# Writing the split parts of 41 weight units to DRAM in the first block and reading them back in the other three

## The chip, the core and the metric

The kernel runs on one core of one Trainium2 chip. The metric is the device time of one execution in microseconds; the time before is 2770.3 us, the median of three runs (2768.29 to 2771.04).

## What is computed

One layer of a streaming encoder on 2048 frames of width 1024, all in float32. One combined projection of the input `h` feeds two branches, which are gated, merged and projected again:

```python
(q_a, k_a, v_a, z_a, beta_a, dec_a, q_b, k_b, v_b, z_b, gate_a, gate_b) = split(h @ w_in)
o_a = gated_deltanet(q_a, k_a, v_a, beta_a, dec_a, conv_w, a_log, dt_bias)   # conv, chunked triangular solve
y_a = rms_norm(o_a) * silu(z_a)
y_b = sliding_window_sink_attention(q_b, k_b, v_b, sinks) * silu(z_b)
mixed = sigmoid(gate_a) * (y_a @ w_proj_a) + sigmoid(gate_b) * (y_b @ w_proj_b)
out = layer_norm(ALPHA * h + mixed @ w_out)
```

The triangular solve of the DeltaNet branch needs, for each pair of heads, the inverse of small lower triangular matrices; the kernel makes it on GpSimd.

## The kernel before

**Tiling.** The 2048 frames are worked in four blocks of 512 columns, one after the other. Each block needs all weights once. A weight unit is 128x1024 float32 (512 KB; the first three of a block, "tm", are a little smaller), and a block uses 93 units in a fixed order, `wlist`: three "tm" units, 38 units of the DeltaNet branch and of the first attention group (convolutions of k, q and v, the z gates, k of the attention), which makes 41, then 12 units of attention, 32 of gates and branch projections and eight of the output projection. The order repeats in every block, and so do loads and splits.

**Split.** A float32 product is made of three fast ones. A unit `wr` is split into a high part `wh` (ScalarE, line 248) and a low part `wl` = `wr` - `wh` (line 142: on VectorE, or on GpSimd for the units in `on_pool`, which all come after the first 41). TensorE then takes `wh` with both parts of the input and `wl` with the high part, 24 matmuls of 512 columns a unit (line 275, 16 with `wh` first, then eight with `wl`).

**Buffers and order.** The pool `wp` has two buffers each for the tags `wr`, `wh` and `wl`. When unit i is taken (`get_w`), the load of unit i+2 is issued on SyncE's queue (SP, line 236), and the split of unit i+1 is begun: ScalarE at once, VectorE three ticks later, a tick being six matmuls. In the first block the k, q and v units also use `wr` itself for the meta tokens (line 281), and their next load is issued in the middle of the unit. All DMAs go through SP's one queue, which issues in program order and stops at a wait.

**What runs beside it.** Two generators are advanced at fixed rates between groups of six matmuls: `chain` (the DeltaNet recurrence, `stage_c`, then attention) and `side` (its preparation, `stage_b0` to `stage_b2`). So the order on every engine is fixed when the program is built. For each of four groups g of two heads, `stage_b1` makes `LT` on VectorE (lines 756 to 763); `inverse` writes pieces of it to DRAM (line 777), reads them back in another layout (781), runs 31 steps of two instructions on GpSimd (789, 791), writes the result to DRAM (797) and reads it back as `XT` (802). `stage_c` starts with a transpose of `XT` on VectorE (854) and matmuls that read it (867, 877). Convolutions are three VectorE instructions (668) with a Tanh on ScalarE (671) and a product (673) behind them. `norm` of the block before (1257, 1259, 1261, 1263) still runs at the start of a block.

Of the kernel before, what the change touches and what calls it, by code (L numbers as in the profile page):

```python
# [11 lines left out]
F32 = mybir.dt.float32  # L12
F32R = mybir.dt.float32r
# [23 lines left out]
CONV = (2, 1, 1)  # L37
DMA = (1, 3, 4, 1, 2, 4)
COLS = 2

GS = (26, 9)
NG = 6
# [4 lines left out]
def weight_order(nblk):  # L47

    fm = lambda *us: [("fm", u) for u in us]
    conv = lambda g: [base + 2 * g + i for base in (U_KA, U_QA, U_VA) for i in range(2)]  # L50
    z = lambda g: [U_ZA + 2 * g, U_ZA + 2 * g + 1]
    swa = lambda kv: [base + 2 * kv + i for base in (U_QB, U_ZB) for i in range(2)]
    r, pool = [], set()
    for b in range(nblk):
        r += [("tm", i) for i in range(3)] + fm(*conv(0), U_KB, U_KB + 1)
        for g in range(4):
            r += fm(*(conv(g + 1) if g < 3 else swa(0)), *z(g))
        n = len(r)
        for kv in range(1, KV):
            r += fm(*swa(kv))  # L60
        for v in range(NG):
            r += fm(U_GA + v, U_GB + v, U_PA + v)
        pool.update(range(n, len(r)))
        r += fm(*(U_PB + v for v in range(NG)))
        for v in range(NG, 8):
            r += fm(U_GA + v, U_GB + v, U_PA + v, U_PB + v)
        r += [("wo", i) for i in range(8)]
    return r, pool
# [3 lines left out]
def hybrid_kernel(  # L72
# [26 lines left out]
    V, A, G, T, SY = nc.vector, nc.scalar, nc.gpsimd, nc.tensor, nc.sync  # L99
    seq = xtok.shape[0]  # L100
    nblk = seq // TB

    cp = ctx.enter_context(tc.tile_pool(name="cp", bufs=1))
    wp = ctx.enter_context(tc.tile_pool(name="wp", bufs=2))
# [6 lines left out]
    dp = ctx.enter_context(tc.tile_pool(name="dp", bufs=1, space=bass.MemoryType.DRAM))  # L111
# [4 lines left out]
    def nm(s):  # L116
        cnt[0] += 1
        return f"{s}_{cnt[0]}"

    def g4(shape, dt=F32):  # L120
        return gp.tile(shape, dt, tag="g", name=nm("g"))
# [17 lines left out]
    f = lambda ap: ap.bitcast(F32)  # L139
    def split_lo(out_, src, hi, pool=False):  # L140
        eng = G if pool else V
        eng.tensor_tensor(out=out_, in0=src, in1=f(hi), op=ALU.subtract)  # L142
# [22 lines left out]


    wlist, on_pool = weight_order(nblk)
    raws, parts = {}, {}
    state = {"dma": 0, "split": 0, "use": 0, "more": 0}

    def w_src(key):
        if key[0] == "tm":
            n = 2 if key[1] == 2 else 3
            return wtm[:, 3 * key[1]:3 * key[1] + n, :], [P, n, 272]
        if key[0] == "wo":
            return wo[key[1] // 4, :, 2 * (key[1] % 4):2 * (key[1] % 4) + 2, :], [P, 2, 512]
        return wfm[key[1]], [P, NK, P]
# [5 lines left out]
    def bg(gen, after=0):  # L183

        if after:
            clock["n"] += 1
            heapq.heappush(waiting, (clock["now"] + after, clock["n"], gen))
            return
        try:
            r = next(gen)  # L190
        except StopIteration:
            return
        if callable(r):
            def poll(r=r):
                while not r():
                    yield 3
                bg(gen)
            bg(poll())
            return
        bg(gen, r)  # L200
# [30 lines left out]
    def next_dma():  # L231
        i = state["dma"]
        if i < len(wlist) and i < state["use"] + state["more"] + 2:
            src, shape = w_src(wlist[i])
            raw = wp.tile(shape, F32, tag="wr", name=nm("wr"))
            SY.dma_start(out=raw, in_=src)
            raws[i] = (raw, shape)
            state["dma"] += 1

    def next_split():  # L240
        i = state["split"]
        if i >= len(wlist) or i >= state["use"] + state["more"] + 1:
            return
        state["split"] += 1
        raw, shape = raws.pop(i)
        keep = i >= len(wlist) - 4
        hi = g4(shape, F32R) if keep else wp.tile(shape, F32R, tag="wh", name=nm("wh"))
        A.activation(hi, raw, AF.Copy)  # L248
        lo = g4(shape, F32R) if keep else wp.tile(shape, F32R, tag="wl", name=nm("wl"))
        parts[i] = (hi, lo, raw)  # L250
        if i in on_pool:
            split_lo(lo, raw, hi, True)
            return
        if i:
            yield LO
        split_lo(lo, raw, hi)

    def get_w(key, keep=False):
        i = state["use"]
        assert wlist[i] == key, (wlist[i], key)  # L260
        state["use"] += 1
        if not keep:
            next_dma()
        bg(next_split())
        hi, lo, raw = parts.pop(i)
        return (hi, lo, raw) if keep else (hi, lo)

    def proj(u, rh, rl, done, meta=None):

        wh, wl, raw = get_w(("fm", u), True) if meta is not None else (*get_w(("fm", u)), None)  # L270
        ps = bank(pa)
        n = 0
        for w_, rs in ((wh, (rh, rl)), (wl, (rh,))):
            for k, r_ in ((k, r_) for k in range(NK) for r_ in rs):
                T.matmul(ps, w_[:, k, :], r_(k), start=(n == 0), stop=(n == 3 * NK - 1))  # L275
                n += 1
                if meta is not None and n == 12:
                    pm = bank(pa)
                    for k_ in range(NK):
                        a = 32 * (k_ % 4)  # L280
                        T.matmul(pm[a:a + 32, :P], f(xm[:, k_, :]), raw[:, k_, :], start=k_ < 4, stop=k_ >= 4, tile_position=(0, a))
                    raw = None
                    next_dma()
                if n % 6 == 0 and n < 3 * NK:
                    yield
# [214 lines left out]
    for q in range(4):  # L500
        for _ in load_x(0, q, nextx, 0):
            pass
        if q < 2:
            next_dma()
        if q == 0:
            xmr = s2([P, NK, NM])
            SY.dma_start(out=xmr, in_=xmT)
            for _ in next_split():
                pass
        if q == 1:  # L510
            A.activation(xm[:, :, 0:NM], xmr, AF.Copy)
            V.tensor_tensor(out=xm[:, :, NM:32], in0=xmr, in1=f(xm[:, :, 0:NM]), op=ALU.subtract)
# [42 lines left out]
    def block(b, nextx):  # L555
# [213 lines left out]
        def inverse(g):  # L769
# [17 lines left out]
            for j in range(31):  # L787
# [3 lines left out]
                G.tensor_tensor(out=X[:, :n, j + 1:], in0=X[:, :n, j + 1:], in1=tm[:, :n, :r], op=ALU.add)  # L791
                if j % COLS == COLS - 1:
                    yield 1
# [431 lines left out]
        def project(nx):  # L1225
# [61 lines left out]
            def half_by_parts(half):  # L1287
                accs = [bank(pa) if half == 0 else bank() for _ in range(NC4)]
                for kq in range(4):
                    wh, wl = get_w(("wo", 4 * half + kq))  # L1290
                    if half == 0 and not last:
                        bg(load_x(b + 1, kq, nx, 6))
                    if last and kq:
                        state["more"] += 1
                        next_dma()
                        bg(next_split())
                    yield from until(lambda: len(mix) > kq)
                    n = 0
                    for lo in (False, True):
                        for k2 in range(2):  # L1300
                            for c in range(NC4):
                                terms(accs[c], c, kq, k2, wh, wl, lo)
                                n += 1 if lo else 2
                                if n % 6 == 0 and (kq, n) != (3, 24):
                                    yield
# [159 lines left out]
```

## Time and profile before

| | before |
|---|---|
| median of three runs | 2770.3 us |
| the profiled execution | 2766.4 us |
| span of its instructions | 2764.6 us |
| TensorE, VectorE, ScalarE, GpSimd busy | 95%, 68%, 48%, 39% |
| starts of the blocks | about 7, 722, 1396 and 2073 us |

Matmuls are pipelined: a matmul of 512 columns is shown with some 400 ns, but the next one starts about 227 ns later, so a busy share of 95% does not say that TensorE is at its peak; what counts is where it stands still, or runs at the lower of its two clock levels. "Idle before" and "waited for" tell how long an engine stood still before an instruction, and which instruction ended that. The chain of work goes back from the last instruction, at each step to what released it.

### The profile page before, as it was taken

The numbers are of one execution on the slowest core, as the hardware profiler recorded it, in microseconds if no ns is written. First come the engines' busy times: TensorE is split into PE (matmuls) and PEld (weight loads), VectorE is DVE, ScalarE is ACT, GpSimd is POOL, SyncE is SP. The second block draws the span as 40 slices with busy tenths as digits, with TensorE's granted clock in tenths as the row PEclk, the third lists the DMA queues.
The fourth block names the chain that finished last, engine by engine and source line by source line (L and its number), as shares of the span: only waits on it lengthen the run. The fifth ranks groups of instructions, "written<-read, shape, count | busy, mean of one in ns | idle before, by whom it ended". The sixth has DMA issues, their size and how long they took to land.

```text
span 2764.6 us, 43948 instructions
## 1 busy us (share of the span) xinstructions
PE 2636.6 (95%) x15308; PEld 2196.2 (79%) x15308; DVE 1869.9 (68%) x4203; ACT 1334.8 (48%) x3337; POOL 1070.7 (39%) x1709
## 2 busy tenths in 40 slices
PE   8999999999989999999997999999999899999997
PEld 6777788888877888788886888878887788878886
DVE  6878868734776767873476675885349677587436
ACT  4555546533355655552344565554224456465422
POOL 2444423431165443443035544444204555344322
PEclk9999999999999999999998999999999899999999
DMA  3322334424433233433443223343353323344233
GB/s 123 91 67 68 92 86 126 121 86 151 138 96 84 75 107 103 132 103 95 154 137 105 77 76 97 111 135 96 99 167 126 90 75 92 95 122 138 85 96 129
DMA packets 196572, 293.49 MB, mean 106 GB/s; under 512 B 72792, under 2 KB 130800, under 8 KB 196352
## 3 DMA queue, kind: packets, MB, share of 16 engines
q1 hardware_dynamic: 196352, 290.70, 35.9%
q8 instruction: 121, 1.98, 0.3%
q14 instruction: 99, 0.81, 0.1%
HBM read 269.59 MB, written 21.02 MB: 105 GB/s over the span
## 4 chain that ended last, share of the span: by engine, by line
PE 67%; DVE 19%; POOL 4%; ACT 4%; issue 3%; DMA 2%; SPq 1%; DVEq 0%; ACTq 0%; POOLq 0%
PE acc L275 46%; DVE s L668 4%; DVE wl L142 2%; POOL tm L789 2%; PE ps L1087 2%; POOL X L791 2%; PE ps L1052 1%; DVE g L673 1%; DVE g L1116 1%; DVE g L763 1%; PE ps L918 1%; PE acc L1346 1%; PE acc L1349 1%; PE acc L1348 1%; PE ps L926 1%
## 5 line engine op out<-in xcount | busy, mean ns | idle before, releaser
L275 PE MATMUL acc<-xh,wh 128*128 128x512 f32 x2112 | 872.4, 413 | 0.0
L275 PE MATMUL acc<-xl,wh 128*128 128x512 f32 x2112 | 837.8, 397 | 0.0
L275 PE MATMUL acc<-xh,wl 128*128 128x512 f32 x2112 | 567.0, 401 | 9.3 <-DVE wl L142 9.1
L248 ACT ACTIVATE wh<-wr 128x1024 fp32r<-128x1024 f32 (+1 forms) x368 | 386.1, 1049 | 304.7 <-PE acc L275 164.9
L142 POOL TENSOR_TENSOR wl<-wr,wh 128x1024 fp32r<-128x1024 f32 x120 | 293.7, 2447 | 592.2 <-ACT wh L248 531.7
L275 PEld LDWEIGHTS acc<-xh,wl 128*128 128x128 f32 x2112 | 394.0, 192 | 93.5 <-DVE wl L142 13.1
L275 PEld LDWEIGHTS acc<-xh,wh 128*128 128x128 f32 x2112 | 404.1, 191 | 72.0 <-issue 0.6
L275 PEld LDWEIGHTS acc<-xl,wh 128*128 128x128 f32 x2112 | 405.0, 192 | 69.8
L142 DVE TENSOR_TENSOR wl<-wr,wh 128x1024 fp32r<-128x1024 f32 (+2 forms) x248 | 324.4, 1308 | 181.9 <-ACT wh L248 150.4
L789 POOL TENSOR_TENSOR tm<-X,g 128x60 f32<-128x60 f32 (+24 forms) x496 | 204.1, 412 | 240.1 <-DMA g<-d 204.5
L668 DVE SCALAR_TENSOR_TENSOR s<-st,cw,s 128x512 f32<-128x512 f32 x288 | 256.0, 889 | 43.2 <-ACT st L663 36.1
L275 PE MATMUL acc<-y,wh 128*128 128x512 f32 x1024 | 250.0, 392 | 0.0
L275 PEld LDWEIGHTS acc<-y,wh 128*128 128x128 f32 x1024 | 189.1, 188 | 37.2
L791 POOL TENSOR_TENSOR X<-X,tm 128x60 f32<-128x60 f32 (+24 forms) x496 | 199.0, 401 | 38.9
L1197 DVE SCALAR_TENSOR_TENSOR g<-g,acc 128x512 f32<-128x512 f32 x64 | 44.0, 688 | 196.0 <-PE acc L275 195.8
L1204 POOL TENSOR_TENSOR g<-g 128x512 f32<-128x512 f32 x32 | 70.0, 2189 | 273.6 <-DVE g L1197 273.6
L1089 ACT ACTIVATE s<-ps 104x512 fp32r<-104x512 f32 (+2 forms) x128 | 76.6, 598 | 156.0 <-PE ps L1087 154.8
L671 ACT ACTIVATE s<-s 128x512 f32<-128x512 f32 x96 | 60.3, 628 | 152.5 <-DVE s L668 152.5
L1188 ACT ACTIVATE g<-acc,bg__157 128x512 f32<-128x512 f32 x64 | 44.1, 690 | 185.4 <-PE acc L275 185.3
L275 PE MATMUL acc<-y,wl 128*128 128x512 f32 x512 | 129.1, 390 | 0.0
L1261 POOL TENSOR_TENSOR y<-y,y 128x1024 f32<-128x1024 f32 x12 | 31.8, 2654 | 233.3 <-DVE y L1259 233.3
L1064 ACT ACTIVATE g<-g,mn 128x208 f32<-128x208 f32 (+2 forms) x256 | 115.3, 455 | 7.3 <-DVE mn L1054 6.7
(313 smaller groups left out, 4532.2 us busy)
## 6 DMA issues: line engine op xcount, KB each, us to landing
wr<-in_wfm_dram SPq DMA_DIRECT2D x328, 512.0 KB
g<-kd SPq DMA_DIRECT2D x240, 96.0 KB
wr<-in_wo_dram SPq DMA_DIRECT2D x32, 512.0 KB
y<-in_xT_dram SPq DMA_DIRECT2D x16, 512.0 KB
g<-d SPq DMA_DIRECT2D x64, 128.0 KB
y<-in_xtok_dram SPq DMA_DIRECT2D x16, 512.0 KB
g<-in_swab_dram SPq DMA_DIRECT2D x16, 416.0 KB
s<-vd SPq DMA_DIRECT2D x120, 52.0 KB
```

The costliest lines, as they stand in the source:

```text
L142: eng.tensor_tensor(out=out_, in0=src, in1=f(hi), op=ALU.subtract)
L248: A.activation(hi, raw, AF.Copy)
L275: T.matmul(ps, w_[:, k, :], r_(k), start=(n == 0), stop=(n == 3 * NK - 1))
L668: V.scalar_tensor_tensor(out=acc, in0=st[:, 3 - d:TB + 3 - d], scalar=cw[:, s, 3 - d:4 - d], in1=acc, op0=ALU.mult, op1=ALU.add)
L671: A.activation(th, acc, AF.Tanh, scale=0.5)
L789: G.tensor_tensor(out=tm[:, :n, :r], in0=X[:, :n, j:j + 1].to_broadcast([P, n, r]), in1=L[:, j:j + 1, j + 1:].to_broadcast([P, n, r]), op= ...
L791: G.tensor_tensor(out=X[:, :n, j + 1:], in0=X[:, :n, j + 1:], in1=tm[:, :n, :r], op=ALU.add)
L1064: A.activation(Pt[:, ch, rt, s:208], Pt[:, ch, rt, s:208], AF.Exp, scale=-1.0, bias=mn[:, ch, rt:rt + 1], accum_out=ls[:, ch, rt:rt + 1])
L1087: T.transpose(out=pT[0:kt, j * 256 + rt * P:j * 256 + rt * P + P], in_=Pt[:, ch, rt, s + j * kt:s + j * kt + kt], identity=ident)
L1089: A.activation(ph[0:kt], pT[0:kt], AF.Copy)
L1188: A.activation(gt_[u][:, br, :], ps, AF.Tanh, scale=0.5, bias=bg_[:, 8 * br + u:8 * br + u + 1])
L1204: G.tensor_tensor(out=m[:, u % 2, :], in0=t[:, 0, :], in1=t[:, 1, :], op=ALU.add)
```

## The change

In the first block, when one of the first 41 units is taken, `wh` and `wl` are also written to two DRAM tiles (two DMAs of 512 KB on SP). In the blocks after, those units are no longer loaded as `wr` and split: both parts are read from DRAM, in two DMAs, into buffers of the same pool; every third unit uses the two `wr` buffers, the others one `wh` and one `wl`. `next_split` has nothing to do for them. The sizes of pools and the matmuls stay the same.

```diff
+NSAVED = 41
@@ next_dma
             src, shape = w_src(wlist[i])
+            state["dma"] += 1
+            if i >= nw and i % nw < NSAVED:
+                tags = ("wr", "wr") if i % nw % 3 == 0 else ("wh", "wl")
+                both = [wp.tile(shape, F32R, tag=t, name=nm(t)) for t in tags]
+                for part, kept in zip(both, saved[i % nw]):
+                    SY.dma_start(out=f(part), in_=kept)
+                parts[i] = (*both, None)
+                return
@@ next_split
         state["split"] += 1
+        if i >= nw and i % nw < NSAVED:
+            return
@@ get_w
+        hi, lo, raw = parts.pop(i)
+        if i < NSAVED:
+            saved[i] = [dp.tile(list(part.shape), F32, name=nm("ws")) for part in (hi, lo)]
+            for part, kept in zip((hi, lo), saved[i]):
+                SY.dma_start(out=kept, in_=f(part))
         if not keep:
             next_dma()
         bg(next_split())
-        hi, lo, raw = parts.pop(i)
```

Line numbers after the change are 12 to 17 higher: 236 becomes 248 (load of `wr`), with 244 for the loads of saved parts and 279 for the stores; 668 becomes 685, 673 becomes 690, 756 to 763 become 773 to 780, 777 becomes 794 and 1259 becomes 1276.

**VectorE, start of the second block**, from the third convolution of the block to `LT` of the first group of heads. `s` and `st` are a convolution's accumulator and its input, `g` its result (and, in line 763, `LT`), `y` a row block of the output of the block before. Before:

```order
L668 SCALAR_TENSOR_TENSOR s_8107<-st_8105,cw,s_8107 128x512 x3
L142 TENSOR_TENSOR wl_8117<-wr_8059,wh_8115 128x1024
L1259 TENSOR_TENSOR y_7459<-y_7459,y_7798 128x1024
L673 SCALAR_TENSOR_TENSOR g_8157<-s_8147,s_8107 128x512
L668 SCALAR_TENSOR_TENSOR s_8177<-st_8175,cw,s_8177 128x512 x3
L142 TENSOR_TENSOR wl_8191<-wr_8113,wh_8189 128x1024
L673 SCALAR_TENSOR_TENSOR g_8157<-s_8218,s_8177 128x512
L756 TENSOR_SCALAR sk_8129<-sk_8129 128x8
```

The same place on VectorE after the change:

```order
L685 SCALAR_TENSOR_TENSOR s_8259<-st_8257,cw,s_8259 128x512 x3
L1276 TENSOR_TENSOR y_7623<-y_7623,y_7960 128x1024
L690 SCALAR_TENSOR_TENSOR g_8307<-s_8298,s_8259 128x512
L685 SCALAR_TENSOR_TENSOR s_8327<-st_8325,cw,s_8327 128x512 x3
L690 SCALAR_TENSOR_TENSOR g_8307<-s_8367,s_8327 128x512
L773 TENSOR_SCALAR sk_8280<-sk_8280 128x8
```

The rest keeps its order; the two splits between are gone. Over the program VectorE and ScalarE have 123 instructions fewer each (3 x 41), and SP has 205 DMAs more (82 stores, 123 second parts).

**SP's queue, the same stretch of the second block**, where the pieces of `LT` go out (`d`), come back (`g`) and a row of the output is stored. Before:

```order
L236 DMA wr_8264<-in_wfm_dram 128x1024
L777 DMA d_1438_8280<-g_8207 32x8x32 x4
L781 DMA g_8319<-d_1438_8280 32x1024 x4
L236 DMA wr_8325<-in_wfm_dram 128x1024
L1263 DMA out_dram<-y_7461 128x1024
```

After (`ws` are the saved parts in DRAM):

```order
L244 DMA wh_8412<-ws_1039 128x1024
L244 DMA wl_8413<-ws_1040 128x1024
L794 DMA d_1511_8427<-g_8356 32x8x32 x4
L798 DMA g_8465<-d_1511_8427 32x1024 x4
L244 DMA wh_8471<-ws_1178 128x1024
L244 DMA wl_8472<-ws_1179 128x1024
L1280 DMA out_dram<-y_7625 128x1024
```

One load becomes two in the same place. Before, it waited for the split that had read the buffer; now it waits for TensorE's last matmul on the part that was there.

**SP's queue in the first block**, at its first units. After:

```order
L279 DMA ws_502<-wh_410 128x1024
L279 DMA ws_503<-wl_412 128x1024
L248 DMA wr_533<-in_wfm_dram 128x1024
L279 DMA ws_602<-wh_506 128x1024
L279 DMA ws_603<-wl_508 128x1024
L248 DMA wr_645<-in_wfm_dram 128x1024
```

Before there was only a row of line 236 where three stand now: two stores went in ahead of each load.

## Rows read from the trace of the kernel before

**Rows 1.** The page: the span, and the chain that ended last, by engine.

```profile
span 2764.6 us, 43948 instructions
...
PE 67%; DVE 19%; POOL 4%; ACT 4%; issue 3%; DMA 2%; SPq 1%; DVEq 0%; ACTq 0%; POOLq 0%
```

**Rows 2.** Stretches: length, busy PE, PEld, DVE, ACT, POOL; clock, DMA, GB/s.

```profile
721.70:796.00 74.30, 66.24 (x342) 55.79 (x341) 69.36 (x132) 35.71 (x85) 32.44 (x25) 0.95 0.41 130
796.00:850.00 54.00, 45.30 (x282) 36.58 (x281) 31.58 (x59) 25.75 (x69) 32.23 (x66) 0.87 0.33 94
850.00:1048.00 198.00, 195.70 (x1354) 165.75 (x1353) 141.22 (x320) 114.17 (x332) 94.74 (x207) 1.00 0.31 86
1396.30:1471.00 74.70, 66.81 (x351) 56.26 (x351) 69.75 (x132) 36.61 (x90) 32.80 (x25) 0.98 0.41 132
1471.00:1525.00 54.00, 44.24 (x273) 35.46 (x272) 31.18 (x58) 24.66 (x63) 31.62 (x66) 0.87 0.32 90
...
2072.60:2148.00 75.40, 68.87 (x347) 57.80 (x347) 69.86 (x132) 35.48 (x84) 33.50 (x25) 0.93 0.42 133
2148.00:2201.00 53.00, 44.33 (x276) 35.87 (x275) 30.88 (x57) 23.64 (x58) 31.00 (x66) 0.87 0.31 89
```

**Rows 3.** TensorE's waits, 721.7 to 850 us: us in total, times, longest.

```profile
PE ps L867 <- DVE sk L756: 5.0, 1, 5.0
PE ps L719 <- DVE g L822: 3.9, 1, 3.9
PE ps L877 <- DVE Y L872: 3.3, 1, 3.3
PE acc L275 <- DVE wl L142: 2.6, 3, 2.1
```

**Rows 4.** Groups of instructions, 721.7 to 1048 us: the splits.

```profile
L142 DVE TENSOR_TENSOR wl<-wr,wh 128x1024 fp32r<-128x1024 f32 (+2 forms) x40 | 52.4, 1309 | 5.6 <-ACT wh L248 5.6
...
L248 ACT ACTIVATE wh<-wr 128x1024 fp32r<-128x1024 f32 (+1 forms) x40 | 41.9, 1047 | 5.4 <-DVE bs L1285 4.0 <-DMA wr<-in_wfm_dram 1.4
```

**Rows 5.** The chain that ended last, 752 to 850 us: start, us, what.

```profile
754.03 1.23 DVE wl L142
...
770.46 2.94 DVE wl L142
...
780.89 1.22 DVE wl L142
...
802.06 1.29 POOL tm L789
```

**Rows 6.** Instructions in order of time: GpSimd's steps and a split.

```profile
801.29 0.29 POOL L789 TENSOR_TENSOR tm<-X,g 128x60 f32<-128x60 f32 x1
...
801.93 1.23 DVE L142 TENSOR_TENSOR wl<-wr,wh 128x1024 fp32r<-128x1024 f32 x1 [2.21 <-ACT wh L248]
```

**Rows 7.** VectorE in order of time: a split, and the wait for XT.

```profile
746.38 1.22 DVE L142 TENSOR_TENSOR wl<-wr,wh 128x1024 fp32r<-128x1024 f32 x1
...
831.59 0.45 DVE L854 STREAM_TRANSPOSE XN<-XT 128x256 f32<-128x256 f32 x1 [8.84 <-DMA XT<-d]
```

**Rows 8.** A crowded stretch; two pieces of the chain; three load issues, the first use.

```profile
674.00:677.00 3.00, 3.00 (x15) 2.49 (x14) 0.78 (x1) 0.42 (x1) 0.00 (x0) 1.00 1.01 407
...
271.78 4.26 DMA wr<-in_wfm_dram
...
1916.38 112.90 PE acc L275 x498
...
726.44 10.34 SPq L236 DMA_DIRECT2D wr<-in_wfm_dram  x3
...
733.81 0.40 PE L275 MATMUL acc<-xh,wh 128*128 128x512 f32 x1
```

**Rows 9.** First block: ScalarE at the start, and its waits for loads to 365 us.

```profile
19.48 1.06 ACT L248 ACTIVATE wh<-wr 128x1024 fp32r<-128x1024 f32 x1 [2.67 <-DMA wr<-in_wfm_dram]
...
ACT wh L248 <- DMA wr<-in_wfm_dram: 20.2, 10, 5.3
```

More of the change, by code (lines that the diff above doesn't have):

```diff
@@ L167, in hybrid_kernel @@
     wlist, on_pool = weight_order(nblk)
+    nw = len(wlist) // nblk
     raws, parts = {}, {}
+    saved = {}
     state = {"dma": 0, "split": 0, "use": 0, "more": 0}
@@ L237, in next_dma @@
             raws[i] = (raw, shape)
-            state["dma"] += 1
     def next_split():
```

## The prediction

> **What bounds the kernel now.** I read first the share of the chain that ended last, then TensorE's standstill by stretch, then its waits, then the chain in the worst stretch, and last the DMAs. The chain is TensorE for 67%, VectorE for 19% and GpSimd for 4% [rows 1]: TensorE bounds the kernel, and VectorE bounds it where TensorE stands still. The three blocks that change look alike, and each stands still mainly in its first 128 us [rows 2]: in the second block TensorE is not busy for 8.1 us of the first stretch (74.30 - 66.24) and 8.7 us of the next, with a granted clock of 0.95 and 0.87, and for only 2.3 us of the 198 us after that, at 1.00. [...] Over the three blocks the standstill of the early stretches is 16.8 + 17.6 + 15.2 = 49.6 us. In the first of them VectorE is the loaded engine: 69.36 us of 74.30 [rows 2]. TensorE's waits are nearly all for VectorE [rows 3]: for a split itself 2.6 us, for a PSUM bank that line 822 frees 3.9 us, and 5.0 and 3.3 us at the head of the recurrence (867, 877), which needs the inverse. There VectorE itself waited 8.84 us for `XT` to land [rows 7], so that wait belongs to the inverse, and the chain shows it: it runs through VectorE up to `LT`, then through GpSimd's steps, then through the DMAs [rows 5].
>
> **What the change removes.** In each of three blocks 41 splits go: 40 in the stretches read here, 52.4 us of VectorE and 41.9 us of ScalarE [rows 4]. Most of it lies beside TensorE's work and is worth nothing: behind 850 us only 2.3 us of standstill are left. What counts is what stands in the chain. Step one: VectorE has three splits there, 1.23 + 2.94 + 1.22 = 5.4 us [rows 5], and one more of 1.22 us just ahead of that stretch [rows 7], in a queue without gaps: 6.6 us by which `LT`, and so the start of the inverse, moves forward. Step two: a step of GpSimd takes 0.29 us, but one that meets a split takes 1.29 us; the split of rows 6 runs from 801.93 to 803.16 us and the step that starts at 802.06 ends with it [rows 5, 6]. Four steps of the chain stand so, one of them in rows 5 (the others, at 808.51, 814.69 and 820.96 us, take 1.19, 1.20 and 1.26 us in the same view): 4 x 0.94 = 3.7 us. Together 10.3 us a block by which `XT` lands earlier. TensorE's own waits ahead of it (split, bank and the clock they cost, 8.1 us of standstill and 0.05 x 74.3 = 3.7 us of clock) shrink by about the same, since VectorE's backlog is behind them; so TensorE comes to line 867 about as much earlier as `XT` does, and the 5.0 and 3.3 us there, with the low clock beside them, stay. Of the 2.3 us later in each block I count half, 1.2 us. Gain: 3 x (10.3 + 1.2) = 34.5 us.
>
> [...]
>
> **What it adds.** In the three later blocks, one more DMA a unit. DMA engines at full share moved 407 GB/s [rows 8], so a pair of 1.05 MB takes 2.6 us of them, 1.3 us more than before. One load landed 4.3 us after its issue [rows 8]; a pair should land within 4.3 + 1.3 + 0.4 for the second issue = 6.0 us. It waits for TensorE's end of the unit three before, so it is issued when two units are still to run, 10.9 us at least (48 matmuls at 112.90 / 498 = 0.227 us [rows 8]). Tightest is the start of a block: before, loads were issued at 726.4 us or after and the first of these units began at 733.81 [rows 8], 7.4 us. So the loads are hidden, with 1 to 5 us to spare; I take nothing, and if that cover is gone each unit costs what it lands too late. Queued behind a pair that waits on SP are the pieces of `LT`, `XT`, the output rows and k and v of attention; they depend on work of the running unit, and the pair ahead of them waits for the unit before it, so SP is past it by then. In front of them the queue of the DMA engines holds up to 1.3 us more of data: four hops an inverse, of which I count none, at most 3 x 5.2 = 16 us if every hop of the three inverses that bind met a full pair.
>
> In the first block, two stores a unit, 82 in all, ahead of each load: 2 x 0.4 us of issue on SP and 2.6 us of the DMA engines, 3.4 us by which a load lands later if the stores are still in flight. From the fourth unit on they are not, as a rule: a load there is issued when the middle of the unit frees its buffer, and the stores went out a unit earlier. The start is different. ScalarE waited for a load already, 2.67 us before the fourth split [rows 9], with the stores of the units ahead newly in the queue; I count the delay there once, 3.4 us. To 365 us ScalarE waited ten times for a load [rows 9]; if each of these grew by 3.4 us and reached TensorE, the cost would be 34 us. The buffers of `wh` and `wl` are also held until the store has read them, but TensorE holds them longer, to the end of the unit. Between nothing and 34 us I take 3.4, since nine of ten waits fall in units whose stores are over.
>
> **Sum.** 34.5 - 3.4 = 31.1 us. The profiled execution took 2766.4 us, 1.8 more than its span and 3.9 less than the median of the runs: it would take 2735.3 us, and the median 2739 us.
>
> **The rivals.**
> [...]
> 2. *Given back at the inverse.* `LT` needs more than VectorE: matmuls, a product of GpSimd (722) and sums of ScalarE. If one of these is next late, only step two is left: 3 x (3.7 + 1.2) - 3.4 = 11 us, 2759 us; with the hops delayed by the pairs as well (16 us), 2775 us, no change.
> 3. *Slower: the first block pays.* The stores of `wh` and `wl` hold up the loads or the buffers of the 26 units there that use `wr` for the meta tokens, whose loads are issued late: 26 x 3.4 = 88 us against 34.5, 2824 us. It decides once a store lands after TensorE is through with its unit, 5.4 us at least (24 matmuls). [...] Against: at 407 GB/s [rows 8] the two stores take 2.6 us of the DMA engines, half of a unit.
> 4. *It doesn't do what it says:* excluded, the order of the instructions shows the 123 splits gone.
>
> **How the numbers follow.** My forecast 0.52 (2725 to 2752). Rival 1: 0.16. Rival 2: 0.22, of which 0.10 within 0.2% of the time before (5.5 us, about what a measurement of this kernel can tell from no change). Rival 3: 0.10. So faster 0.80, same 0.10, slower 0.10. The range goes from 2700, in the middle of rival 1, to 2768, through most of rival 2; outside lie rival 3, half of rival 1 and the end of rival 2, about 0.2.
>
> **What would show it.** Right: in the early stretches VectorE some 14 us less busy, no wait of TensorE for a split, the bank wait of line 822 (839 after) below 2 us, GpSimd's loop of the first inverse some 4 us shorter, `XT` about 10 us earlier from the block's start, and the wait for it at the recurrence still there. [...] What I know least is what is next late once the splits are gone.

## The result, and the profile after

The changed kernel takes **2724.65 us** (median of 4 runs, 2721.2 to 2725.9) against 2769.39 us for the kernel before on the same chip: a ratio of **0.9836 (95% interval 0.9819 to 0.9853)**, 44.7 us less. The forecast was 2739 us, 31 us less, with a range of 2700 to 2768: the direction and the range held, and the size came out 14 us too small. The page of the profiled execution, the answer to [rows 1] (span; shares of the chain that ended last):

```profile
span 2719.1 us, 44006 instructions
...
PE 75%; DVE 15%; ACT 3%; POOL 3%; DMA 2%; issue 2%; SPq 1%; DVEq 0%; ACTq 0%; POOLq 0%
```

VectorE's share of the chain went from 19% to 15%, GpSimd's from 4% to 3%; TensorE's rose from 67% to 75%. The blocks of the changed kernel start at 6.8, 725.3, 1382.8 and 2041.9 us. So the first is 3.6 us longer than before (718.5 for 714.9), and the others are shorter by 17.1, 17.2 and 14.8 us: together the 45.5 us between the spans. The line of busy times in the page, before and then after, says in what form TensorE has them:

```profile
PE 2636.6 (95%) x15308; PEld 2196.2 (79%) x15308; DVE 1869.9 (68%) x4203; ACT 1334.8 (48%) x3337; POOL 1070.7 (39%) x1709
```

```profile
PE 2622.8 (96%) x15308; PEld 2191.7 (81%) x15308; DVE 1707.3 (63%) x4080; ACT 1221.9 (45%) x3214; POOL 997.6 (37%) x1709
```

Its standstill, span less busy time, fell by 31.7 us (128.0 to 96.3), and its busy time for the same 15308 matmuls by 13.8 us, with a mean granted clock of 0.986 for 0.981. Read in pieces of half a microsecond, that clock is 1.00 or 0.50 in both traces, and between the two only where it changes. In the kernel before it is 0.50 from 829.5 to 836.1 us, and of four matmuls of 512 columns there each starts 0.42 to 0.43 us behind the one ahead. So the mean of a stretch says how much of it ran at the lower clock.

The second block by stretch, the answer to the first three of [rows 2] (length, busy PE, PEld, DVE, ACT, POOL, then clock, DMA share, GB/s):

```profile
725.30:799.60 74.30, 71.21 (x380) 61.19 (x379) 54.98 (x123) 30.38 (x89) 36.22 (x46) 0.98 0.73 240
799.60:853.60 54.00, 49.84 (x333) 41.15 (x332) 30.44 (x60) 23.62 (x73) 26.29 (x61) 0.94 0.51 155
853.60:1035.00 181.40, 181.13 (x1271) 154.04 (x1269) 105.01 (x286) 86.25 (x285) 72.36 (x191) 1.00 0.49 147
```

In the same 74.3 us VectorE is busy for 54.98 us, not 69.36, and TensorE does 380 matmuls there, not 342. The DMA engines moved 240 GB/s in place of 130, and still no wait of TensorE for a load shows up in the later blocks. TensorE's waits in the whole execution at the places of [rows 3], first after (the recurrence's lines are now 884 and 894, the bank's 736; 739, now 756, transposes the result of a convolution), then before (us in total, times, longest):

```profile
PE ps L894 <- issue: 11.0, 3, 4.0
PE ps L756 <- DVE g L690: 9.9, 3, 5.6
PE ps L736 <- DVE g L839: 9.1, 3, 3.1
...
PE ps L884 <- DVE sk L773: 3.3, 2, 1.7
```

```profile
PE ps L867 <- DVE sk L756: 16.6, 3, 6.4
PE ps L739 <- DVE g L673: 15.0, 13, 3.8
PE ps L877 <- DVE Y L872: 12.3, 9, 3.3
PE acc L275 <- DVE wl L142: 9.1, 8, 2.1
PE ps L719 <- DVE g L822: 8.5, 3, 3.9
```

The reader should see four things: the waits for a split (9.1 us) are gone, the wait at the head of the recurrence fell from 16.6 to 3.3 us, the next wait (877, now 894) and the bank's wait stayed, and the wait at 739 for VectorE's convolution went from the later blocks. It was 2.5 to 2.6 us in each of them; all 9.9 us after the change, and 7.5 of the 15.0 us before, lie in the first block.

**Two ways to see one block's gain.** TensorE does the same work from the second block's start to the recurrence's first product, and it takes 97.0 us in place of 110.4; in the third block 97.1 in place of 110.4. Those stretches, before and then after:

```profile
721.70:832.10 110.40, 97.05 (x493) 80.82 (x491) 84.89 (x152) 54.57 (x141) 58.38 (x80) 0.96 0.37 115
1396.30:1506.70 110.40, 95.72 (x491) 79.72 (x490) 85.12 (x152) 54.35 (x140) 58.34 (x80) 0.98 0.37 114
```

```profile
725.30:822.30 97.00, 93.91 (x491) 79.93 (x489) 65.46 (x139) 42.66 (x128) 50.48 (x80) 0.98 0.66 214
1382.80:1479.90 97.10, 92.46 (x491) 78.80 (x489) 64.52 (x137) 41.94 (x127) 50.47 (x80) 1.00 0.66 212
```

For the same matmuls (the trace before shows two records more in the second block) TensorE is busy 3.1 and 3.3 us less (at a granted clock of 0.98 and 1.00 for 0.96 and 0.98), and idle 10.3 and 10.0 us less: 13.35 to 3.1, and 14.7 to 4.6. Seen from the inverse, `XT` is taken up by VectorE 95.4 us behind the block's start (820.69 - 725.3), before 109.9 us (831.59 - 721.7, [rows 7]): 14.5 us earlier (13.3 and 13.5 us in the third and fourth block). VectorE waits 3.69 us for it now, not 8.84; in the other two blocks 6.4 us, not 10.4 and 9.0:

```profile
820.69 0.45 DVE L871 STREAM_TRANSPOSE XN<-XT 128x256 f32<-128x256 f32 x1 [3.69 <-DMA XT<-d]
```

Where those 14.5 us come from: the loop of GpSimd starts 7.4 us earlier from the block's start (first step 65.3 us before, 57.9 us after; 7.3 and 7.6 us in the other two blocks), and it is 6.9 us shorter (6.0 us in the other two). GpSimd's steps in the second block's first inverse, before and then after (duration min/median/max in ns, first and last start):

```profile
L789 POOL TENSOR_TENSOR tm<-X,g x31: 213/303/1283, 787.0 to 823.5; 128x60 f32<-128x60 f32 x3, 128x28 f32<-128x28 f32 x2, 128x54 f32<-128x54 f32 x2, 128x48 f32<-128x48 f32 x2
L791 POOL TENSOR_TENSOR X<-X,tm x31: 219/305/1192, 787.6 to 823.8; 128x60 f32<-128x60 f32 x3, 128x28 f32<-128x28 f32 x2, 128x54 f32<-128x54 f32 x2, 128x48 f32<-128x48 f32 x2
```

```profile
L806 POOL TENSOR_TENSOR tm<-X,g x31: 213/299/702, 783.2 to 812.8; 128x60 f32<-128x60 f32 x3, 128x28 f32<-128x28 f32 x2, 128x54 f32<-128x54 f32 x2, 128x48 f32<-128x48 f32 x2
L808 POOL TENSOR_TENSOR X<-X,tm x31: 219/303/854, 783.6 to 813.1; 128x60 f32<-128x60 f32 x3, 128x28 f32<-128x28 f32 x2, 128x54 f32<-128x54 f32 x2, 128x48 f32<-128x48 f32 x2
```

From the first step's start to the last's 36.8 us before, 29.9 us after. The median of a step is nearly the same; the longest are gone (longest 1283 and 1192 ns, now 702 and 854).

### The profile page after: what moved, and what is told of

Same layout as the page of the kernel before. It is cut to its first block, busy times and chain, and to the rows that moved or that the text cites. A ratio compares the mean times of both kernels' runs of the same rounds, so it can differ in the third digit from the quotient of the medians.

```text
span 2719.1 us, 44006 instructions
## 1 busy us (share of the span) xinstructions
PE 2622.8 (96%) x15308; PEld 2191.7 (81%) x15308; DVE 1707.3 (63%) x4080; ACT 1221.9 (45%) x3214; POOL 997.6 (37%) x1709
## 4 chain that ended last, share of the span: by engine, by line
PE 75%; DVE 15%; ACT 3%; POOL 3%; DMA 2%; issue 2%; SPq 1%; DVEq 0%; ACTq 0%; POOLq 0%
PE acc L292 52%; DVE s L685 3%; PE ps L1104 2%; PE ps L1069 1%; POOL X L808 1%; POOL tm L806 1%; PE ps L935 1%; PE ps L956 1%; PE ps L943 1%; PE ps L924 1%; PE ps L945 1%; PE acc L1363 1%; PE acc L1366 1%; PE acc L1365 1%; DVE g L1133 1%
## 5 line engine op out<-in xcount | busy, mean ns | idle before, releaser
L292 PE MATMUL acc<-xh,wh 128*128 128x512 f32 x1800 | 743.1, 413 | 0.0
L292 PE MATMUL acc<-xl,wh 128*128 128x512 f32 x1800 | 713.6, 396 | 0.0
L292 PE MATMUL acc<-xh,wl 128*128 128x512 f32 x1800 | 477.9, 397 | 0.0
L292 PEld LDWEIGHTS acc<-xh,wh 128*128 128x128 f32 x1800 | 344.5, 191 | 60.9 <-issue 0.6
L292 PEld LDWEIGHTS acc<-xl,wh 128*128 128x128 f32 x1800 | 345.1, 192 | 59.1
L292 PEld LDWEIGHTS acc<-xh,wl 128*128 128x128 f32 x1800 | 332.3, 190 | 67.5 <-issue 0.5
L261 ACT ACTIVATE wh<-wr 128x1024 fp32r<-128x1024 f32 (+1 forms) x245 | 258.0, 1053 | 280.4 <-PE acc L292 164.9
L144 DVE TENSOR_TENSOR wl<-wr,wh 128x1024 fp32r<-128x1024 f32 (+2 forms) x125 | 165.9, 1327 | 156.0 <-ACT wh L261 137.1
L292 PE MATMUL acc<-xh,wr 128*128 128x512 f32 x624 | 211.5, 406 | 0.0
L292 PEld LDWEIGHTS acc<-xh,wr 128*128 128x128 f32 x624 | 118.0, 191 | 23.7
```

## The experiments

Twelve runs (after_again is the changed kernel once more, low_again is low_only once more), each measured beside the kernel before on its own chip:

| run | median, us | ratio to before (95%) | against before, us |
|---|---|---|---|
| first14 | 2729.0 | 0.9858 (0.9845 to 0.9871) | -38.8 |
| last26 | 2759.5 | 0.9968 (0.9956 to 0.9980) | -8.3 |
| stores_only | 2768.8 | 1.0005 (0.9996 to 1.0013) | +1.0 |
| back_one | 2735.3 | 0.9888 (0.9872 to 0.9905) | -32.0 |
| back_three | 2752.6 | 0.9947 (0.9933 to 0.9960) | -14.6 |
| back_two | 2772.8 | 1.0020 (1.0011 to 1.0028) | +5.0 |
| back_four | 2784.7 | 1.0061 (1.0048 to 1.0074) | +17.0 |
| low_only | 2717.1 | 0.9826 (0.9811 to 0.9840) | -50.2 |
| after_again | 2719.7 | 0.9831 (0.9818 to 0.9845) | -48.1 |
| low_again | 2716.2 | 0.9815 (0.9801 to 0.9828) | -51.6 |
| y_on_act | 2720.3 | 0.9832 (0.9817 to 0.9846) | -47.0 |
| low_y | 2761.7 | 0.9981 (0.9972 to 0.9989) | -6.1 |

### Which units give the gain

first14 keeps 14 units in place of 41:

```
-NSAVED = 41
+NSAVED = 14
```

> Only the first 14 weight units of a block are kept and read back, 15 to 41 are split anew as before. My theory: the gain is made while the triangular inverse waits in VectorE's queue and in the GpSimd loop, so in the first 14 units of a block: of the 16.4 us that a later block lost on average, 14.5 (block 1, up to XT) stay. First block pays a third of 3.6 us or a little more: 2769.4 - 3 x 14.5 + 2 = about 2728 us (2722 to 2736), within 0.3% of the changed kernel. Rival, the gain is spread over all kept units because TensorE or a DMA was waited for everywhere: 14 of 41 of 49 us, 2769.4 - 17 + 1 = about 2754 us.

last26 keeps units 15 to 40 alone, counted from 0 (unit 14 is kept in neither run):

```
-            if i >= nw and i % nw < NSAVED:
+            if i >= nw and LOW <= i % nw < NSAVED:
...
-        if i < NSAVED:
+        if LOW <= i < NSAVED:
```

> Only units 15 to 40 of a block (counted from 0) are kept and read back, the first 15 are split anew as before. My theory: after XT a later block lost 2.6 us, so 3 x 2.6 less and some 2 us more in the first block: 2769.4 - 8 + 2 = about 2763 us (2757 to 2770), and the GpSimd loop of a later block stays at 38 us. Rival, the gain is spread evenly: 26 of 41 of 49 us less, about 2740 us.

Measured: 38.8 us less for the first 14, 8.3 us less for 26 of the others; together 47.1, which is the changed kernel's gain (44.7 and 48.1 in its two comparisons). The even spread, 16 and 29 us, is excluded. In last26 GpSimd's loop is 35.9 us long (790.8 to 826.7), nearly as before; in first14 it starts as early as in the changed kernel and takes 31.7 us (778.2 to 809.9). So a third of the DRAM room and of the stores buys four fifths of the gain: what counts are the splits ahead of the block's first inverse and beside it.

### What the stores cost

```
+        hi, lo, raw = parts.pop(i)
+        if i < NSAVED:
+            for part in (hi, lo):
+                SY.dma_start(out=dp.tile(list(part.shape), F32, name=nm("ws")), in_=f(part))
```

> The kernel before, with the stores of the high and low parts of 41 units added in the first block; nothing reads them, every later block makes its splits anew. It measures the cost term alone. By the comparison of the two profiles 3.6 us in the first block and nothing later: 2769.4 + 3.6 = 2773 us (2771 to 2776). Rival, the stores cost more and the later blocks had hidden it: 2780 us or more. A third way: the 3.6 us are not the stores but the waits of the tiles that they hold, which would show as well here, on the release of the weight tiles.

The time is 1.0 us above the kernel before, between 1.1 less and 3.6 more, a little under what I expected (1.6 to 6.6 more). The first block of the profiled execution is 720.4 us long, 5.5 more than before, and the later ones 1.9 us shorter in sum. In the kernels that store both parts and are otherwise the same in the first block, it took 715.7 to 720.4 us; in the two that store the low parts alone, 711.5 and 715.4 us; before, 714.9 us. So a first block with all the stores takes some 3.5 us more on average, and one of the same instructions moves by as much from one execution to the next: the 3.6 us of the result are near what can be seen at all. Rival 3 of the prediction, 88 us, is far off.

### Is it VectorE's time, or its second operand?

A split costs VectorE time, 1.22 us, and it reads two SBUF tiles; a step of GpSimd beside it took 1.29 us for 0.29 [rows 5, 6], and these rows do not tell which of the two lengthens the step. Four kernels put back VectorE work that nothing uses, into blocks 2 to 4, at the places of the splits that are gone; the loads, the freed ScalarE and TensorE's missing dependence on the split stay as in the changed kernel.

back_one, a maximum with one operand:

```
         if i >= nw and i % nw < NSAVED:
+            hi, lo, _ = parts[i]
...
+            yield LO
+            V.tensor_reduce(out=jr, in_=f(hi), op=ALU.max, axis=AX.XY)
             return
```

> The changed kernel, and in blocks 2 to 4 each kept unit gets one useless instruction back on VectorE at the place where its split stood, with one SBUF operand: a maximum over the 1024 columns of the high part, about as long as the split. It gives back VectorE's time. [...] Theory B, the loop is shorter because VectorE's own steps in it come earlier, whatever the operands: it goes back to 36 to 38 us, and the time to 2760 us or more, as the variant with two operands.

back_two, subtractions with two operands:

```
...
+            n, w = hi.shape[1:]
+            step = max(1, 256 // w)
+            for j in range(0, n, step):
...
+                V.tensor_tensor(out=o_, in0=f(hi[:, j:j + step]), in1=f(lo[:, j:j + step]), op=ALU.subtract, saturate=False)
```

> The changed kernel, and in blocks 2 to 4 each kept unit gets a useless subtraction back on VectorE, at the place where its split stood: two SBUF operands, 1024 columns in four instructions of 256, into a small tile that nothing reads. ScalarE stays free of the copies and TensorE doesn't wait for the result. My theory, VectorE's queue (6.6 us a block) and the sharing with GpSimd (6.7 us) are the whole gain: it goes back to 2769.4 + 3.6 = 2773 us less what TensorE no longer waits for splits (2 us a block), so 2762 to 2775. Rival, the gain came from ScalarE's copies or TensorE's waits for splits: it stays at 2725 to 2740.

back_two went to 2772.8 us, as my theory had it, but it is a poor proof: its four instructions a unit held VectorE for 39.4 us in the first 150 us of the second block, where the splits had taken 24.4 us and the maximum of back_one 24.7. So two more runs, one with as much VectorE time and one operand, one with the second operand at about the dose of the splits, going by the median of an instruction.

back_four, four maxima of 416 columns:

```
...
+            for part in (hi, lo):
+                for j in range(0, n, 4):
+                    V.tensor_reduce(out=jr, in_=f(part[:, j:min(j + 4, n), :104]), op=ALU.max, axis=AX.XY)
```

> The control for the variant with the useless subtractions, which gave VectorE more time back than the splits had taken (39.4 us in the first 150 us of a block, where the splits took 24.4): four useless maxima per kept unit, of 416 columns each and one SBUF operand, about 0.5 us each, so as many instructions and about as much VectorE time as there, and no second operand. If the second operand is what slows GpSimd, the GpSimd loop stays at 30 us (30.2 with one maximum, 32.3 to 33.7 with the subtractions) and the time lies between: 2735 for the single maximum, and some 6 us a block for the longer queue ahead of the inverse, 2754 us (2746 to 2760). If VectorE's time alone made the difference between 2735 and 2773, it comes to 2768 to 2778 us.

back_three, three of the four subtractions:

```
-            for j in range(0, n, step):
+            for j in range(0, min(n, 6), step):
```

> The useless subtractions at the dose of the splits: three of the four instructions of 256 columns per kept unit, 3 x 0.425 us by their median, 1.28 us against 1.21 us of the single maximum and 1.22 us of a split. So it differs from the variant with one maximum (2735 us) in the second SBUF operand and little else. If the second operand is what GpSimd and VectorE pay for, the GpSimd loop takes 32 us or more (30.2 with the maximum), VectorE's instructions have a mean well above their median, and the time is 2750 to 2765 us. If it isn't, 2733 to 2742 us, and the gain is VectorE's queue and TensorE's waits for the splits themselves.

The loop of GpSimd in the three that tell most, back_one, back_three and back_four in this order:

```profile
L811 POOL TENSOR_TENSOR tm<-X,g x31: 214/302/738, 788.0 to 817.8; 128x60 f32<-128x60 f32 x3, 128x28 f32<-128x28 f32 x2, 128x54 f32<-128x54 f32 x2, 128x48 f32<-128x48 f32 x2
L813 POOL TENSOR_TENSOR X<-X,tm x31: 223/309/722, 788.7 to 818.1; 128x60 f32<-128x60 f32 x3, 128x28 f32<-128x28 f32 x2, 128x54 f32<-128x54 f32 x2, 128x48 f32<-128x48 f32 x2
```

```profile
L814 POOL TENSOR_TENSOR tm<-X,g x31: 213/312/702, 790.2 to 821.2; 128x60 f32<-128x60 f32 x3, 128x28 f32<-128x28 f32 x2, 128x54 f32<-128x54 f32 x2, 128x48 f32<-128x48 f32 x2
L816 POOL TENSOR_TENSOR X<-X,tm x31: 220/321/778, 790.9 to 821.5; 128x60 f32<-128x60 f32 x3, 128x28 f32<-128x28 f32 x2, 128x54 f32<-128x54 f32 x2, 128x48 f32<-128x48 f32 x2
```

```profile
L813 POOL TENSOR_TENSOR tm<-X,g x31: 210/297/702, 796.3 to 825.9; 128x60 f32<-128x60 f32 x3, 128x28 f32<-128x28 f32 x2, 128x54 f32<-128x54 f32 x2, 128x48 f32<-128x48 f32 x2
L815 POOL TENSOR_TENSOR X<-X,tm x31: 217/308/799, 796.9 to 826.2; 128x60 f32<-128x60 f32 x3, 128x28 f32<-128x28 f32 x2, 128x54 f32<-128x54 f32 x2, 128x48 f32<-128x48 f32 x2
```

**GpSimd's loop** takes 30.1 us with one operand (788.0 to 818.1) and 29.9 us with one operand and far more VectorE time (796.3 to 826.2): the 29.9 us of the changed kernel, whose third and fourth blocks have 30.9 and 31.0. VectorE's time alone does not lengthen it. With the second operand, in pieces of 256 columns, it takes 31.3 us, a little less than I expected and hardly more than the changed kernel's own loops, so these pieces are not shown to lengthen it; with the splits, which hold 1024 columns at once, it takes 36.8 us. In back_one a maximum stands beside four steps of the loop, and none is much longer than the same step of the changed kernel with no VectorE instruction beside it: 0.38, 0.31, 0.32 and 0.31 us, there 0.35, 0.31, 0.32 and 0.31 us (the view is the instructions in order of time: start, us):

```profile
801.63 0.38 POOL L813 TENSOR_TENSOR X<-X,tm 128x76 f32<-128x76 f32 x1
...
801.72 1.21 DVE L261 TENSOR_REDUCE jr<-wr 128x1 f32<-128x1024 f32 x1
...
802.10 0.31 POOL L811 TENSOR_TENSOR tm<-X,g 128x72 f32<-128x72 f32 x1
...
802.49 0.32 POOL L813 TENSOR_TENSOR X<-X,tm 128x72 f32<-128x72 f32 x1
...
802.89 0.31 POOL L811 TENSOR_TENSOR tm<-X,g 128x68 f32<-128x68 f32 x1
```

Beside a split, in the kernel before, one step of 128x76 took 1.29 us and ended with the split [rows 5, 6]. **VectorE's instructions can take longer as well**: ahead of the inverse GpSimd makes two products of 1024 columns. Beside the first the maximum of back_one takes its 1.21 us, while in back_three the three subtractions, beside both products, take 4.52 us, where 3 x 0.425 us (their median) would be 1.28. Here the pieces lose more than GpSimd, whose first product takes 2.19 us for 1.92 in back_one: in the first 150 us of the second block the 59 subtractions of back_three hold VectorE for 33.9 us, where 59 medians would be 25.1, and `LT` is done 57.3 us behind the block's start, in back_one 54.3. The lines, back_one first:

```profile
757.36 1.21 DVE L261 TENSOR_REDUCE jr<-wr 128x1 f32<-128x1024 f32 x1
757.36 1.92 POOL L730 TENSOR_TENSOR g<-cm,gh 128x1024 fp32r<-128x1024 f32 x1 [2.44 <-DVE gh L644]
```

```profile
757.13 2.19 POOL L733 TENSOR_TENSOR g<-cm,gh 128x1024 fp32r<-128x1024 f32 x1 [2.45 <-DVE gh L647]
757.13 4.52 DVE L264 TENSOR_TENSOR jk<-wr,wr 128x256 fp8e4<-128x256 f32 x3
759.28 2.09 POOL L733 TENSOR_TENSOR g<-cm,gl 128x1024 fp32r<-128x1024 f32 x1
```

What it means for the time: one operand at the dose of the splits costs 48.1 - 32.0 = 16 us of the gain (13 us against the first comparison), the second operand, in three instructions for one, another 32.0 - 14.6 = 17 us, and 15 us are left even then. Behind these last stand TensorE's 9.1 us of waits for splits, and splits of 1024 columns where back_three has pieces of 256; I did not separate the two, so what the second operand costs in whole splits is not shown as a time. For one operand I had estimated 20 us, step one's 6.6 us in three blocks, so 2738 to 2752 us with a loop near 31 us. back_one came out 3 us below the least of that: its maxima cost 13 to 16 us, and the loop takes 30.1 us.

back_four contradicts my number: 2785 us, not 2754, though its loop is short. With 42.5 us of maxima in the first 150, VectorE's load shows in TensorE's waits directly. The longest:

```profile
PE ps L763 <- DVE g L697: 29.6, 13, 5.7
PE ps L743 <- ACT junk L852: 20.5, 3, 7.3
```

Of the first, 17.9 us lie in the later blocks, where the changed kernel has no such wait (its 9.9 us at line 756 are all in the first block). So of the 37 us between back_one and back_two the larger part came from the dose, the 20 us behind back_three; the 17 us between back_one and back_three are the operands' price, in pieces of 256 columns.

### Does ScalarE's relief matter?

low_only stores and reads back the low parts alone; ScalarE makes the high parts from the raw weights in every block:

```
         parts[i] = (hi, lo, raw)
+        if i >= nw and i % nw < NSAVED:
+            SY.dma_start(out=f(lo), in_=saved[i % nw])
+            return
...
```

> Only the low parts of the 41 units are kept and read back; the high parts are copied from the raw weights by ScalarE in every block, as before. VectorE is relieved as in the changed kernel, ScalarE isn't, and a load moves half the bytes more than before rather than twice. My theory, the gain is VectorE's alone: 2725 us (2719 to 2732). Rival, ScalarE's copies were half of it: 2740 to 2750 us.

It is no slower: 2717.1 us, 2 us below what I expected. The 41.9 us of ScalarE in each block [rows 4] were worth nothing. Since it moves fewer bytes, I put it beside the changed kernel on one chip, both as they are.

> The changed kernel as it is, beside the variant that keeps the low parts alone, on the same chip: 2718 to 2727 us, as a yardstick for its difference.

> The variant that keeps only the low parts, once more beside the changed kernel. It measured 2717.1 us against 2724.7 in other comparisons. If half the stores and a third less loading are worth something (the first block was 715.4 us there and 718.5 in the changed kernel), it is 3 to 7 us below the changed kernel here; if the two were only different chips, within 2 us of it.

2716.2 against 2719.7 us, 3.5 us less, inside the expected 3 to 7; but the intervals of the two ratios still overlap (0.9801 to 0.9828, and 0.9818 to 0.9845). It is the best kernel of the study, with half the DRAM room, probably a little ahead of the changed kernel; that is not settled. Its loads are not quite hidden: TensorE waits 1.3 us (low_only) and 2.2 us (low_again) in all for a low part to land.

### The wait that is left at the recurrence

TensorE still waits 3.5 to 4.0 us a block at 894, for the copies of `Y`: the view names no releaser there, but in the second block the first product starts at 829.99 us, as the first of two copies that take 0.88 us from 829.47 ends. y_on_act gives them to ScalarE:

```
-                V.tensor_copy(Y[bq:bq + 32], py[bq:bq + 32, 0:256].rearrange("p (m i) -> p m i", m=8))
+                A.activation(Y[bq:bq + 32], py[bq:bq + 32, 0:256].rearrange("p (m i) -> p m i", m=8), AF.Copy)
```

> The changed kernel, with the two copies of Y from PSUM in stage_c made by ScalarE in place of VectorE. TensorE waits 3.5 to 4.0 us a block for them, since they stand behind VectorE's preparation of the next group. If that wait goes: 3 to 4 us less in each of four blocks, 2724.7 - 14 = about 2711 us (2708 to 2718). Rival, the copies now stand behind ScalarE's evictions, or the next step waits for VectorE anyway: 2722 to 2730 us, with a wait of TensorE of the same length at the next line.

The rival was right. The time is the changed kernel's, and the wait is as long. The wait, and the chain behind it:

```profile
PE ps L894 <- ACT Y L889: 4.1, 1, 4.1
```

```profile
824.20 0.76 DVE s L685
...
824.99 0.63 ACT s L688
...
825.64 0.38 ACT Y L889
```

ScalarE has the copies behind line 688, which waits for VectorE's convolution (685), so they stand behind the same work as before. low_y, on top of low_only, has the copies on ScalarE too, and emits the product and the copies without the step in between:

```
             A.activation(N64[32:64, :, 32:64], XN[32:64], AF.Copy)
-            yield
-
             py = bank()
...
```

> The variant that keeps only the low parts, with the two copies of Y on ScalarE and emitted right behind the two copies of N64, without the step in between in which VectorE's preparation of the next group came ahead (in the earlier variant the copies on ScalarE stood behind a ScalarE instruction that waited for that preparation, 4.1 us as before). Hope: TensorE's wait of 3.5 to 4.0 us a block at the next line goes, 10 to 14 us less than the variant without. Rival: the product that makes Y now stands some 4 us earlier in TensorE's order, ahead of XN, and TensorE waits there for about as long: 0 to 4 us less.

45 us slower than low_only, far outside both. TensorE now waits for `XN` (first fence: low_y; second: the same places in low_again, whose wait for `XN` does not show):

```profile
PE ps L875 <- DVE XN L864: 24.1, 8, 4.2
...
PE ps L875 <- DVE sk L766: 9.1, 3, 4.4
```

```profile
PE ps L887 <- DVE Y L882: 5.9, 5, 1.9
PE ps L877 <- DVE sk L766: 4.5, 3, 1.6
```

33.2 us of waits took the place of 10.4; that is half of the loss. The two pages show 14.3 us more of TensorE's busy time (2635.2 us for 2620.9), and the rest lies in smaller waits that I did not follow. I had worked the wait out for one group of heads, and the order changed for every group.

## Why the prediction was right, point by point

**The place and the mechanism were right.** The gain is in the early stretches; VectorE is 14.4 us less busy there (forecast some 14); TensorE no longer waits for a split; the loads are hidden; `XT` lands earlier. That the first block costs 3.6 us (forecast 3.4) is luck: I placed the cost at the fourth split, but the 1500th matmul starts 0.3 us earlier than before (224 us in) and the 2500th 3.8 us later (371 us in), and stores_only put the stores at 1.0 us.

**Step one, VectorE's queue ahead of `LT`:** forecast 6.6 us a block. `LT` is done 6.5 us earlier, and the loop starts 7.4 us earlier (65.3 to 57.9). The one-operand run splits this up: in back_one the loop starts at 63.0 us, so 5.1 us of it are VectorE's time. Of the other 2.3 us, 1.7 are what the split of 2.94 us [rows 5] took beyond its usual 1.22.

**Step two, GpSimd's steps beside splits: the term that was mis-sized.** Forecast 3.7 us a block, from four steps at 0.94 us; the loop is 6.9 us shorter in the second block, 6.0 in the other two. The four steps gave their part: 0.96, 0.86, 0.90 and 1.02 us, 3.7 us. I had counted only steps that meet a split. The steps in all take 5.4 us less, since the convolutions (668) and the products behind them (673), which also read two tiles, now fall beside fewer steps of the loop: beside 17 of 62 before (steps beside a split not counted), with a median of 0.66 us, and beside 13 after, with 0.69 us, where a step beside no VectorE instruction has 0.29 and 0.30 us. My sum had left them where they were. The remaining 1.5 us are gaps between steps (10.1 to 8.5 us). That a step beside a split is longer was right, the row that I counted was too narrow.

**The waits at the recurrence: the step that failed.** I argued that TensorE comes there as much earlier as `XT` does, so that the 5.0 and 3.3 us stay. In the second block `XT` came 14.5 us earlier. TensorE on its own side came only 8.4 us earlier: its waits ahead of the product fell from 8.35 to 3.1 us, and its busy time by 3.1 us. So the wait at 867 went almost entirely, 16.6 to 3.3 us over three blocks, and with it part of the low clock (0.87 in the stretch before; 0.94, 0.91 and 0.90 in the three blocks after). The second wait, at 877, stayed, since it hangs on VectorE's work behind `XN` and not on the inverse. So about half of the two waits went, in place of my own "stays". That brought no gain beyond `XT`'s, though: the product starts 13.4 us earlier, 1.1 less than `XT`, because there TensorE is now the later of the two.

The low end of my range, 2700 us, supposed that both waits, 8.3 us a block, and the low clock beside them go almost whole. No run shows that: over the three blocks the changed kernel still waits 11.0 us at 894, and the clock of the stretch went to 0.94, 0.91 and 0.90, not to 1.00.

**The bank's wait** (719, now 736): forecast below 2 us, measured 3.1 in the second block and 9.1 over three, before 3.9 and 8.5. It went on without the splits.

**The later part** of a block: forecast 1.2 us, measured 2.6, 3.8 and 1.3 us behind `XT`.

**The sum:** the three later blocks gave 17.1 + 17.2 + 14.8 = 49.1 us in place of 34.5, the first block took 3.6 in place of 3.4. Of the 14.6 us too many, some 10.5 are `XT` (14.5, 13.3 and 13.5 us earlier, forecast 10.3 each), which is step two above all, and 4.1 the later part.

## What to carry to other kernels

Where VectorE and GpSimd work side by side, look for both prices in the trace. Here a split, with two SBUF operands, cost its own 1.22 us, and each of four steps beside one took some 0.94 us more, while a maximum with one operand lengthened its four steps by 0.03 us at most. Cutting the instruction into pieces moved this price more than it removed it: beside the pieces of back_three GpSimd's loop took 31.3 us for 29.9, but they took 33.9 us of VectorE for 25.1. A cached split pays where it stands in the queue ahead of a serial chain, or beside one: 14 units of 41 gave four fifths of the gain, and the part that only relieved ScalarE gave nothing. When a step shortens a chain and the engine that waits for it has a path of its own, work out both arrivals apart: here 14.5 and 8.4 us, and the difference ate the wait (in the other two blocks, most of it).

## What the runs showed of the hardware

- A small VectorE instruction can take long beside GpSimd. In the changed kernel a product of 128x8 takes 1.58 us beside a GpSimd product of 1.92 us, where the instruction ahead of it, with one operand of the same size, takes 0.20 us. The next one, a multiplication by a constant with one operand, takes 1.84 us beside GpSimd's second product, so two operands are not the only case. The median of either over the kernel is 0.17 us, and both are as long in each later block (1.53 and 1.84 us in the third, 1.58 and 1.83 us in the fourth). They stand in VectorE's queue ahead of the copies of `Y`: some 3.1 us of the wait at 894 that is left. Moving them was not tried:

```profile
821.23 0.20 DVE L774 RECIPROCAL cj<-sk 128x8 f32<-128x8 f32 x1
821.46 1.58 DVE L775 TENSOR_TENSOR cj<-cj,gm4be 128x8 f32<-128x8 f32 x1
823.07 1.84 DVE L776 TENSOR_SCALAR ncj<-cj 128x8 f32<-128x8 f32 x1
```

```profile
821.10 1.92 POOL L725 TENSOR_TENSOR g<-cm,gh 128x1024 fp32r<-128x1024 f32 x1
822.97 1.92 POOL L725 TENSOR_TENSOR g<-cm,gl 128x1024 fp32r<-128x1024 f32 x1
```

- Beside smaller pieces GpSimd's steps were shorter. With 256 columns at a time (back_three, second block) no step of GpSimd's loop took over 0.78 us, no more than the 0.85 us of the changed kernel without any; with the splits' 1024 up to 1.28 us.
- 82 more stores, nearly all of 512 KB, in the first block cost 1.0 us of time (1.1 less to 3.6 more). The first block of stores_only moved 158 GB/s, that of the kernel before 101:

```profile
7.00:727.40 720.40, 692.32 (x4250) 566.91 (x4251) 494.93 (x1266) 345.23 (x926) 248.84 (x426) 0.98 0.49 158
```
